# One output projection pass for two mixers, and x added in the attention instead of before it

## The chip, the cores and the metric

The kernel runs on one core of one Trainium2 chip. The metric is the device time of one execution in microseconds (us), less is better. The core's engines are PE (TensorE, matmuls), DVE (VectorE), ACT (ScalarE), POOL (GpSimd) and SP (SyncE, which issues most DMA transfers). Each engine runs its own list of instructions in order and waits on semaphores for the others.

## What is computed

One layer of a hybrid backbone: a modulated norm, one input projection into three mixers (A, differential attention; B, gated linear attention; C, neighbourhood attention), one output projection with a gated residual, a second norm, a mixture of experts and a final norm. What matters here is the residual around the mixers:

```
ya, _ = diff_attention(...)            # 512 columns
yb, _ = gla_mixer(...)                 # 256 columns
yn, _ = neighborhood_attention(...)    # 256 columns
x = x + mod[:, 2] * (jnp.concatenate([ya, yb, yn], axis=-1) @ w_out)
h2 = rms_norm(x, g2) * (1 + mod[:, 4]) + mod[:, 3]
f = hier_moe(h2.reshape(-1, D), w_rg, b_rg, w_re, b_re, w_up, w_down)
x = x + mod[:, 5] * f.reshape(B_, S, D)
return rms_norm(x, final_g)
```

There are 1024 tokens of 1024 numbers, so 8 token tiles of 128 rows. `w_out` is 1024x1024: rows 0 to 511 belong to A, 512 to 767 to B, 768 to 1023 to C.

## The kernel before

**Stages.** Modulation and input projection, mixer B, mixer C, the output projection of B and C (`gen_o`), the attention A with its own part of the output projection, norm, router and token ranking per tile, then the experts, then the final norm. Up to the attention a scheduler sets the order on every engine by what is ready. In the attention and the experts the order on PE, DVE and ACT is written out by hand; SP and POOL stay scheduled there.

**float32 on PE.** Each operand is split into a high and a low part (names in h and l: `mh`, `ml`, `whh`, `whl`), and each product takes three matmuls: high times high, low weight times high, high weight times low.

**The projection before.** `gen_o` (L1066) runs twice. The first run takes mixer B's rows (`mixB`, in the trace `rbm`) with the weights `wB` (`wh`, `wl`, prepared early), the second mixer C's (`mixC`) with `wC` (`whh`, `whl`). In each, per token tile: ACT casts `mh` (L1073), DVE makes `ml` (L1074), and for each of two column halves n PE runs 2 x 3 matmuls of 128x512 (L1079 to L1081) into one of three PSUM buffers `pj`, which DVE adds into `x1` (L1082). `x1` is one SBUF tile of 32 KB per partition that holds x for all 8 tiles, loaded by eight DMAs (L1120) near the end of mixer C. In the second run ACT issues the write of each finished tile to `X1` in device memory (L1084).

**wC.** `wout(768)` (L1053) loads two raw tiles of 512 KB into memory that mixer C has to leave first; for each DVE multiplies by the gate (L1062), ACT casts the high part (L1037), DVE subtracts for the low part (L1034).

**Mixer C's end.** L994 (`cpo`) are its value matmuls, L981 its transposes, L997 the copies into `mixC`.

**The attention.** Units of (tile t, head h), 32 in all. One unit: scores S on PE (L1271, L1272), the row maximum `nm` on DVE (L1273), the exponentials on ACT (L1278), the update of p on DVE (L1284), transposes on PE, values on PE. Work of earlier tiles is woven in with fixed lags: `mixt` loads that tile's X1 rows into `x1t` and forms `mh` and `ml` of A; `proj` (tiles 0 to 6) or `proj_heads` (tile 7) multiplies by A's part of `w_out` and adds into `x1t` (L1368 for tile 7); then the norm, written to `H2` (L1407, POOL), the router, `choose` (small DVE steps up to the one-hot `oh`, L1476), and `rank` (PE, L1488, which reads `oh`). The 30 first steps are a loop; the end is a list written by hand. Buffers named `h2` (in the trace `h`) hold a tile's norm; there are two.

Of the kernel before, what the change touches and what calls it, by code (L numbers as in the profile page):

```python
# [18 lines left out]
D = 1024  # L19
# [3 lines left out]
NT = 8  # L23
# [44 lines left out]
def body(nc, tc, d, tap=None, upto=None):  # L68
# [997 lines left out]
    def gen_o(rows_of, hi, lo, last=False):  # L1066

        o1, x1 = late["o1"], late["x1"]
        for t in range(NT):
            mix = rows_of(t)  # L1070
            mh = o1.tile([128, 2, 128], F32R, name="mh", bufs=2)
            ml = o1.tile([128, 2, 128], F32R, name="ml", bufs=2)
            nc.scalar.copy(mh, mix)  # L1073
            eng(ENG[15]).tensor_sub(ml, mix, mh.bitcast(F32))  # L1074
            for n in range(2):
                cs = slice(512 * n, 512 * n + 512)
                ps = pj.tile([128, 512], F32, name="pj")
                for k in range(2):
                    nc.tensor.matmul(ps, lhsT=mh[:, k, :], rhs=hi[:, k, cs], start=(k == 0), stop=False)  # L1079
                    nc.tensor.matmul(ps, lhsT=mh[:, k, :], rhs=lo[:, k, cs], start=False, stop=False)  # L1080
                    nc.tensor.matmul(ps, lhsT=ml[:, k, :], rhs=hi[:, k, cs], start=False, stop=(k == 1))  # L1081
                nc.vector.tensor_add(x1[:, t, cs], ps, x1[:, t, cs])  # L1082
                if last and n:
                    nc.scalar.dma_start(X1[t * 128:(t + 1) * 128, :], x1[:, t, :])  # L1084
                yield 1.3
# [16 lines left out]
    def last_steps():  # L1102
# [15 lines left out]
        late["x1"] = x1 = O1.enter_context(tc.tile_pool(name="x1", bufs=1)).tile([128, NT, D], F32, name="x1")  # L1118
        for t in range(NT):
            dmab(x1[:, t, :], d["x"][t * 128:(t + 1) * 128, :])  # L1120
# [34 lines left out]
    run(gen_o(lambda t: mixB[:, t], *late["wB"]))  # L1155
    run(gen_o(lambda t: mixC[:, :, t * 128:(t + 1) * 128], *wC, True))
# [6 lines left out]
    if upto == "o1":  # L1163
        nc.sync.dma_start(d["out"], X1)
        A.__exit__(None, None, None)
        Xp.__exit__(None, None, None)
        ctx.close()
        return
# [140 lines left out]
    class Til:  # L1309
# [25 lines left out]
        def mixt(self, a=0, b=4):  # L1335
            if a == 0:
                self.x1 = w2.tile([128, D], F32, name="x1t", bufs=BX1)
                dmab(self.x1, X1[self.t * 128:(self.t + 1) * 128, :])
            pt = apt()
# [14 lines left out]
        def proj_heads(self, ps, n, k0, k1):  # L1354
            cs = slice(512 * n, 512 * n + 512)
            for k in range(k0, k1):
# [14 lines left out]
        def proj(self, n, ps=None):  # L1371
            ps = apt()[:, :256] if ps is None else ps
            cs = slice(256 * n, 256 * n + 256)
# [793 lines left out]
```

## Time and profile before

| what | us |
|---|---|
| median of three runs | 1674.91 (1671.81 to 1677.38) |
| the profiled execution | 1675.7 |
| its span, first to last instruction | 1673.9 |
| mean granted PE clock, as a share of 2.4 GHz | 0.944 |
| PE busy | 1462.1 (87%) |
| DVE busy | 1233.5 (74%) |
| ACT busy | 999.1 (60%) |
| POOL busy | 546.2 (33%) |

The busy shares are means over stages. The projection lies at about 563 to 634 us, the attention at 634 to 930, the experts from about 948 on. The rows that follow further down are from these stretches.

### The profile page before, as it was taken

The numbers are of one execution on the slowest core, as the hardware profiler recorded it, in microseconds if no ns is written. First come the engines' busy times: TensorE is split into PE (matmuls) and PEld (weight loads), VectorE is DVE, ScalarE is ACT, GpSimd is POOL, SyncE is SP. The second block draws the span as 40 slices with busy tenths as digits, with TensorE's granted clock in tenths as the row PEclk, the third lists the DMA queues.
The fourth block names the chain that finished last, engine by engine and source line by source line (L and its number), as shares of the span: only waits on it lengthen the run. The fifth ranks groups of instructions, "written<-read, shape, count | busy, mean of one in ns | idle before, by whom it ended". The sixth has DMA issues, their size and how long they took to land. (4 is left out here: it accounts for less than half of the span.)

```text
span 1673.9 us, 24624 instructions
## 1 busy us (share of the span) xinstructions
PE 1462.1 (87%) x8611; PEld 1193.7 (71%) x8611; DVE 1233.5 (74%) x1936; ACT 999.1 (60%) x1602; POOL 546.2 (33%) x608
## 2 busy tenths in 40 slices
PE   6899799899989897999998689988999999999840
PEld 2698677777777776899998567666777777777730
DVE  5713657965544365867787689998999999999957
ACT  4624546754434523767664377766777777777742
POOL 0201423222322203377885413322222223233224
PEclk9999899999988897999999799999999999999975
DMA  9324572106543686222227789887999999999344
GB/s 325 102 58 137 163 227 67 49 27 186 128 109 96 200 268 244 77 65 89 64 89 273 274 302 337 317 306 261 335 349 344 342 343 344 339 347 340 144 179 192
DMA packets 163502, 353.18 MB, mean 211 GB/s; under 512 B 28247, under 2 KB 83735, under 8 KB 163376
## 3 DMA queue, kind: packets, MB, share of 16 engines
q1 hardware_dynamic: 139552, 307.87, 53.4%
q0 software_dynamic: 22096, 37.94, 7.4%
q10 hardware_dynamic: 1728, 5.78, 0.9%
q8 instruction: 69, 1.13, 0.3%
q14 instruction: 57, 0.47, 0.1%
HBM read 318.30 MB, written 49.30 MB: 220 GB/s over the span
## 5 line engine op out<-in xcount | busy, mean ns | idle before, releaser
L1832 DVE TENSOR_TENSOR wlo<-wraw,whi 128x1024 fp32r<-128x1024 f32 x384 | 505.8, 1338 | 42.8 <-ACT whi L1831 37.7
L1831 ACT CAST whi<-wraw 128x1024 fp32r<-128x1024 f32 x384 | 399.5, 1049 | 160.7 <-PE epu L1859 110.3
L1858 PE MATMUL epu<-wlo,xh 128*128 128x512 f32 x512 | 210.4, 411 | 44.0 <-DVE wlo L1832 42.7
L1857 PE MATMUL epu<-whi,xh 128*128 128x512 f32 x512 | 208.4, 407 | 2.2 <-ACT xh L1849 2.2
L1859 PE MATMUL epu<-whi,xl 128*128 128x512 f32 x512 | 203.9, 398 | 1.0 <-DVE xl L1850 1.0
L1858 PEld LDWEIGHTS epu<-wlo,xh 128*128 128x128 f32 x512 | 97.1, 190 | 89.5 <-DVE wlo L1832 69.3
L1836 POOL DMA_INDIRECT xg<-H,gidx x30 | 42.2, 1407 | 332.2 <-PE ept L1847 320.6
L1877 POOL TENSOR_TENSOR y<-y,m 128x1024 f32<-128x1024 f32 x31 | 88.8, 2865 | 136.2 <-ACT y L1876 136.2
L1273 DVE TENSOR_REDUCE nm<-S 128x1 f32<-128x1280 f32 x64 | 94.9, 1489 | 51.0 <-PE S L1272 42.4
L385 PE MATMUL pj<-wh,hh 128*128 128x256 f32 (+1 forms) x384 | 114.8, 299 | 1.3 <-ACT kbT L342 1.3
L1857 PEld LDWEIGHTS epu<-whi,xh 128*128 128x128 f32 x512 | 97.4, 190 | 24.0 <-ACT xh L1849 2.8
L387 PE MATMUL pj<-wh,hl 128*128 128x256 f32 (+1 forms) x384 | 113.3, 295 | 0.0
L386 PE MATMUL pj<-wl,hh 128*128 128x256 f32 (+1 forms) x384 | 113.3, 295 | 0.0
L1859 PEld LDWEIGHTS epu<-whi,xl 128*128 128x128 f32 x512 | 97.3, 190 | 22.3 <-DVE xl L1850 1.7
L1857 PE MATMUL epy<-whi,ah 128*128 128x512 f32 x256 | 109.0, 426 | 2.3 <-ACT y L1876 2.3
L1858 PE MATMUL epy<-wlo,ah 128*128 128x512 f32 x256 | 102.9, 402 | 0.7 <-DVE wlo L1832 0.7
L1859 PE MATMUL epy<-whi,al 128*128 128x512 f32 x256 | 102.3, 400 | 0.0
L374 PE MATMUL pj<-hh,wh 128*128 128x512 f32 (+1 forms) x240 | 99.9, 416 | 0.0
L1278 ACT ACTIVATE p<-S,nm 128x1280 f32<-128x1280 f32 x64 | 84.6, 1331 | 21.2 <-DMA x1t<-w_out 15.4
L375 PE MATMUL pj<-hl,wh 128*128 128x512 f32 (+1 forms) x240 | 92.1, 384 | 0.0
L376 PE MATMUL pj<-hh,wl 128*128 128x512 f32 (+1 forms) x240 | 91.9, 383 | 0.0
L1271 PE MATMUL S<-ak,aq 128*128 128x512 f32 (+1 forms) x192 | 76.1, 397 | 10.8 <-ACT p L1278 10.0
(447 smaller groups left out, 3513.6 us busy)
## 6 DMA issues: line engine op xcount, KB each, us to landing
wraw<-w_up SPq DMA_DIRECT2D x254, 512.0 KB
wraw<-w_down SPq DMA_DIRECT2D x127, 512.0 KB
wm<-w_mod SPq DMA_DIRECT2D x32, 512.0 KB
raw<-w_in SPq DMA_DIRECT2D x22, 512.0 KB
wm<-w_mod SPq DMA_DIRECT2D x32, 256.0 KB
aq<-QS SPq DMA_DIRECT2D x64, 128.0 KB
wraw<-YS SPq DMA_DIRECT2D x16, 512.0 KB
ak<-KS SPq DMA_DIRECT2D x8, 640.0 KB
```

The lines of the kernel that those rows point to most:

```text
L374: nc.tensor.matmul(ps[:, :n], lhsT=a, rhs=x, start=(k == 0), stop=False)
L375: nc.tensor.matmul(ps[:, :n], lhsT=a, rhs=y, start=False, stop=False)
L376: nc.tensor.matmul(ps[:, :n], lhsT=b, rhs=x, start=False, stop=(k == 7))
L385: nc.tensor.matmul(ps[:, :n], lhsT=a, rhs=wh[:, k, :], start=(k == 0), stop=False)
L386: nc.tensor.matmul(ps[:, :n], lhsT=a, rhs=wl[:, k, :], start=False, stop=False)
L387: nc.tensor.matmul(ps[:, :n], lhsT=b, rhs=wh[:, k, :], start=False, stop=(k == 7))
L1273: V.tensor_reduce(u.nm[:, m:m + 1], sv, axis=AX.X, op=OP.max, negate=True)
L1831: nc.scalar.copy(hi, raw)
L1832: nc.vector.tensor_sub(lo, raw, hi.bitcast(F32))
L1857: nc.tensor.matmul(ps[:, cs], lhsT=ah[:, k, :], rhs=hi[:, cs], start=(k == 0), stop=False)
L1858: nc.tensor.matmul(ps[:, cs], lhsT=ah[:, k, :], rhs=lo[:, cs], start=False, stop=False)
L1859: nc.tensor.matmul(ps[:, cs], lhsT=al[:, k, :], rhs=hi[:, cs], start=False, stop=(k == nk - 1))
```

## The change

The two runs of `gen_o` become one. Per token tile it casts both mixers' rows (`mh` and `ml` are now 128x4x128), and per column half PE runs four steps of three matmuls into one PSUM buffer: two steps with wB, two with wC. The result is copied to a new tile `ev` (two buffers), by ACT for n = 0 and by DVE for n = 1, and ACT writes `ev` to X1. The `x1` tile and its eight loads are gone, so X1 holds the projection without x. In the attention `mixt` loads x of the tile into a buffer of the name `h2` (`xx`), and DVE adds it to `x1t` ahead of the first projection column block: in `proj` for tiles 0 to 6, in `proj_heads` for tile 7. An early exit for tests (`upto == "o1"`) is dropped. In the changed kernel the three matmul lines of `gen_o` are L1083 to L1085, the copies L1086, the write L1087, the adds L1371 (`proj`) and L1351 (`proj_heads`); lines of the attention above them move by a few numbers (L1273 to L1265, L1284 to L1276, L1476 to L1474).

```
-    def gen_o(rows_of, hi, lo, last=False):
-
-        o1, x1 = late["o1"], late["x1"]
+    def gen_o(wB, wC):
+
+        o1 = late["o1"]
         for t in range(NT):
-            mix = rows_of(t)
-            mh = o1.tile([128, 2, 128], F32R, name="mh", bufs=2)
-            ml = o1.tile([128, 2, 128], F32R, name="ml", bufs=2)
-            nc.scalar.copy(mh, mix)
-            eng(ENG[15]).tensor_sub(ml, mix, mh.bitcast(F32))
+            mh = o1.tile([128, 4, 128], F32R, name="mh", bufs=2)
+            ml = o1.tile([128, 4, 128], F32R, name="ml", bufs=2)
+            for z, mix in enumerate((mixB[:, t], mixC[:, :, t * 128:(t + 1) * 128])):
+                zs = slice(2 * z, 2 * z + 2)
+                nc.scalar.copy(mh[:, zs], mix)
+                eng(ENG[15]).tensor_sub(ml[:, zs], mix, mh[:, zs].bitcast(F32))
+            ev = o1.tile([128, D], F32, name="ev", bufs=2)
             for n in range(2):
                 cs = slice(512 * n, 512 * n + 512)
                 ps = pj.tile([128, 512], F32, name="pj")
-                for k in range(2):
-                    nc.tensor.matmul(ps, lhsT=mh[:, k, :], rhs=hi[:, k, cs], start=(k == 0), stop=False)
-                    nc.tensor.matmul(ps, lhsT=mh[:, k, :], rhs=lo[:, k, cs], start=False, stop=False)
-                    nc.tensor.matmul(ps, lhsT=ml[:, k, :], rhs=hi[:, k, cs], start=False, stop=(k == 1))
-                nc.vector.tensor_add(x1[:, t, cs], ps, x1[:, t, cs])
-                if last and n:
-                    nc.scalar.dma_start(X1[t * 128:(t + 1) * 128, :], x1[:, t, :])
-                yield 1.3
+                for k in range(4):
+                    hi, lo = (wB, wC)[k // 2]
+                    h, l = hi[:, k % 2, cs], lo[:, k % 2, cs]
+                    nc.tensor.matmul(ps, lhsT=mh[:, k, :], rhs=h, start=(k == 0), stop=False)
+                    nc.tensor.matmul(ps, lhsT=mh[:, k, :], rhs=l, start=False, stop=False)
+                    nc.tensor.matmul(ps, lhsT=ml[:, k, :], rhs=h, start=False, stop=(k == 3))
+                (nc.vector.tensor_copy if n else nc.scalar.copy)(ev[:, cs], ps)
+            nc.scalar.dma_start(X1[t * 128:(t + 1) * 128, :], ev)
...
-        late["x1"] = x1 = O1.enter_context(tc.tile_pool(name="x1", bufs=1)).tile([128, NT, D], F32, name="x1")
-        for t in range(NT):
-            dmab(x1[:, t, :], d["x"][t * 128:(t + 1) * 128, :])
...
-    run(gen_o(lambda t: mixB[:, t], *late["wB"]))
-    run(gen_o(lambda t: mixC[:, :, t * 128:(t + 1) * 128], *wC, True))
+    gen_o(late["wB"], wC)
...
                 self.x1 = w2.tile([128, D], F32, name="x1t", bufs=BX1)
                 dmab(self.x1, X1[self.t * 128:(self.t + 1) * 128, :])
+                self.xx = w2.tile([128, D], F32, name="h2", bufs=BH2)
+                dmab(self.xx, d["x"][self.t * 128:(self.t + 1) * 128, :])
...
         def proj_heads(self, ps, n, k0, k1):
             cs = slice(512 * n, 512 * n + 512)
+            if k0 == n == 0:
+                V.tensor_add(self.x1, self.x1, self.xx)
...
         def proj(self, n, ps=None):
             ps = apt()[:, :256] if ps is None else ps
             cs = slice(256 * n, 256 * n + 256)
+            if n == 0:
+                V.tensor_add(self.x1, self.x1, self.xx)
```

**PE at the end of mixer C.** The names: `cpo` is mixer C's output, `wh` and `wl` are wB, `whh` and `whl` are wC, `mh` and `ml` the mixers' rows, `pj` the PSUM buffers. The kernel before:

```order
L1079 MATMUL pj_5813<-wh_5063,mh_5801 128x512
L1080 MATMUL pj_5813<-wl_5064,mh_5801 128x512
L994 MATMUL cpo_5718<-cpT_5708,vw_5582 64x128
L994 MATMUL cpo_5718<-cpT_5716,vw_5582 64x128
L1081 MATMUL pj_5813<-wh_5063,ml_5802 128x512
L994 MATMUL cpo_5718<-cpT_5708,vw_5582 64x128
L994 MATMUL cpo_5718<-cpT_5716,vw_5582 64x128
L1079 MATMUL pj_5825<-wh_5063,mh_5821 128x512
L994 MATMUL cpo_5718<-cpT_5708,vw_5582 64x128
L994 MATMUL cpo_5718<-cpT_5716,vw_5582 64x128
L1080 MATMUL pj_5825<-wl_5064,mh_5821 128x512
L1081 MATMUL pj_5825<-wh_5063,ml_5822 128x512
```

The same place in the changed kernel:

```order
L994 MATMUL cpo_5706<-cpT_5696,vw_5570 64x128
L994 MATMUL cpo_5706<-cpT_5704,vw_5570 64x128
L1083 MATMUL pj_5776<-whh_5723,mh_5769 128x512
L1083 MATMUL pj_5790<-whh_5723,mh_5769 128x512
L1083 MATMUL pj_5812<-whh_5723,mh_5805 128x512
L1084 MATMUL pj_5776<-whl_5724,mh_5769 128x512
L1085 MATMUL pj_5776<-whh_5723,ml_5770 128x512
L1083 MATMUL pj_5776<-whh_5723,mh_5769 128x512
```

Before, B matmuls of one PSUM buffer after another stand between and behind mixer C's last matmuls; now the first projection matmuls behind them read wC, and 18 B matmuls stand further ahead, in both programs.

**DVE in a unit of the attention.** `nm` is the row maximum and factor, `p0` the probabilities, `fm`, `eid`, `oh`, `tB` belong to `choose` of an earlier tile. The kernel before:

```order
L1284 SCALAR_TENSOR_TENSOR p0_7715<-p1_7717,nm_7680,p0_7715 128x1280
L1469 TENSOR_TENSOR fm_7747<-fm_7747,iot_5519 128x32
L1472 TENSOR_SCALAR fm_7747<-fm_7747,eid_5522 128x32
L1473 TENSOR_SCALAR oh0_7870<-iot_5519,eid_5522 128x32
L1449 ISA fm_7747,eid_5522<-fm_7747 128x32
L1449 ISA eid_5522 128x1
L1475 TENSOR_SCALAR tB0_7872<-iot_5519,eid_5522,cid_6178 128x32
L1476 TENSOR_SCALAR oh1_7871<-iot_5519,eid_5522 128x32
L1273 TENSOR_REDUCE nm_7894<-S0_6195 128x1
```

The same place in the changed kernel, where the tile's x lies in `h2_7719`:

```order
L1276 SCALAR_TENSOR_TENSOR p0_7671<-p1_7673,nm_7636,p0_7671 128x1280
L1371 TENSOR_TENSOR x1t_7717<-x1t_7717,h2_7719 128x1024
L1467 TENSOR_TENSOR fm_7703<-fm_7703,iot_5519 128x32
L1470 TENSOR_SCALAR fm_7703<-fm_7703,eid_5522 128x32
L1471 TENSOR_SCALAR oh0_7829<-iot_5519,eid_5522 128x32
L1447 ISA fm_7703,eid_5522<-fm_7703 128x32
L1447 ISA eid_5522 128x1
L1473 TENSOR_SCALAR tB0_7831<-iot_5519,eid_5522,cid_6125 128x32
L1474 TENSOR_SCALAR oh1_7830<-iot_5519,eid_5522 128x32
```

The add stands between the update of p and the steps that end with `oh`. It stands so for tiles 2 to 5; for tiles 0 and 1 no `choose` step follows it, and for tile 6 it stands between the maxima and the update of p.

**SP at the attention's end.** `x1t` is tile 7's load of X1, `wraw` are raw weights of the experts, `h2` in the changed kernel tile 7's x. The kernel before:

```order
L77 DMA x1t_9248<-X1_68 128x1024
L1894 DMA wraw_9629<-w_down 128x1024
L1894 DMA wraw_9631<-w_down 128x1024
L1894 DMA wraw_9633<-w_down 128x1024
L1894 DMA wraw_9635<-w_down 128x1024
L1894 DMA wraw_9637<-w_up 128x1024
```

The changed kernel:

```order
L77 DMA x1t_9216<-X1_68 128x1024
L1892 DMA wraw_9600<-w_down 128x1024
L1892 DMA wraw_9602<-w_down 128x1024
L1892 DMA wraw_9604<-w_down 128x1024
L1892 DMA wraw_9606<-w_down 128x1024
L77 DMA h2_9218<-x 128x1024
L1892 DMA wraw_9608<-w_up 128x1024
```

The load of tile 7's x stands behind four loads of `w_down` and ahead of the next of `w_up`.

## Rows read from the trace of the kernel before

**Rows 1.** Timeline of PE at the end of mixer C and in the projection: start in us, busy us, engine, line, operation, output<-inputs, tile and shape, count, and in brackets the idle time before and what ended it. Between the rows of 591.83 and 600.03 stand 34 more matmuls of this kind.

```profile
557.52 0.77 PE L981 MATMUL cps<-ident,cs 128*128 128x128 f32 x5
563.46 0.79 PE L1079 MATMUL pj<-wh,mh 128*128 128x512 f32 x1 [5.17 <-ACT mh L1073]
...
588.16 0.50 PE L1079 MATMUL pj<-wh,mh 128*128 128x512 f32 x1
...
591.12 0.44 PE L994 MATMUL cpo<-cpT,vw 128*64 128x128 f32 x4
...
591.83 0.40 PE L1081 MATMUL pj<-wh,ml 128*128 128x512 f32 x1
...
600.03 0.40 PE L1080 MATMUL pj<-wl,mh 128*128 128x512 f32 x1
...
603.18 0.47 PE L1079 MATMUL pj<-wh,mh 128*128 128x512 f32 x1 [1.31 <-DVE x L1082]
...
633.00 0.40 PE L1081 MATMUL pj<-whh,ml 128*128 128x512 f32 x1
```

**Rows 2.** Waits of SP's queue from 585 to 606 us (line, what it waited for: us in total, times, longest) and, from the timeline of SP, the issue that ended the wait.

```profile
SPq L77 <- PE cpo L994: 7.9, 1, 7.9
...
591.72 0.81 SPq L77 DMA_DIRECT2D raw<-w_out  x2
```

**Rows 3.** Timeline of DVE from mixer C's last copy to the attention's first maxima, columns as in rows 1.

```profile
591.61 0.29 DVE L997 COPY mixC<-cpo 128x128 f32<-128x128 f32 x1 [0.16 <-PE cpo L994]
...
595.78 0.69 DVE L1082 TENSOR_TENSOR x<-pj,x 128x512 f32<-128x512 f32 x1 [0.39 <-PE pj L1081]
596.39 1.22 DVE L1062 TENSOR_TENSOR raw<-raw 128x1024 f32<-128x1024 f32 x1
...
598.12 1.22 DVE L1062 TENSOR_TENSOR raw<-raw 128x1024 f32<-128x1024 f32 x1
...
601.20 1.23 DVE L1034 TENSOR_TENSOR whl<-raw,whh 128x1024 fp32r<-128x1024 f32 x1
...
633.44 0.69 DVE L1082 TENSOR_TENSOR x<-pj,x 128x512 f32<-128x512 f32 x1 [0.71 <-PE pj L1081]
641.83 2.89 DVE L1273 TENSOR_REDUCE nm<-S 128x1 f32<-128x1280 f32 x2 [7.70 <-DMA X<-x]
```

**Rows 4.** Timeline of ACT: the first cast of wC, and the last three issues of X1 writes (one row, its time is that of all three with the waits between them).

```profile
597.68 1.06 ACT L1037 CAST whh<-raw 128x1024 fp32r<-128x1024 f32 x1 [0.33 <-DVE raw L1062]
...
628.54 5.97 ACTq L1084 DMA_DIRECT2D X<-x  x3
```

**Rows 5.** Windows of the projection and of the attention's start: from:to and length in us, then busy us and instruction count of PE, PE's weight loads, DVE, ACT and POOL, the granted PE clock as a share of 2.4 GHz, the share of DMA busy, and GB/s.

```profile
560.00:564.00 4.00, 0.55 (x1) 0.50 (x2) 1.08 (x4) 2.91 (x8) 1.75 (x4) 0.70 0.57 132
592.00:596.00 4.00, 4.00 (x18) 3.22 (x18) 1.93 (x4) 0.41 (x1) 0.00 (x0) 1.00 0.69 254
600.00:604.00 4.00, 1.99 (x8) 1.02 (x7) 3.57 (x6) 1.17 (x2) 0.00 (x0) 1.00 1.10 347
636.00:640.00 4.00, 0.78 (x5) 0.48 (x3) 0.00 (x0) 0.00 (x0) 1.08 (x1) 1.00 1.02 420
640.00:644.00 4.00, 0.00 (x0) 0.00 (x0) 2.17 (x2) 0.60 (x1) 0.00 (x0) 0.51 1.03 418
644.00:660.00 16.00, 11.94 (x37) 9.83 (x38) 9.58 (x8) 6.41 (x11) 9.34 (x4) 0.50 0.67 244
...
656.00:660.00 4.00, 4.00 (x17) 3.62 (x16) 1.13 (x2) 1.41 (x3) 0.00 (x0) 0.50 0.42 172
660.00:664.00 4.00, 4.00 (x30) 3.70 (x30) 3.04 (x5) 3.97 (x8) 0.00 (x0) 0.93 0.00 0
```

**Rows 6.** Window of one unit in the middle of the attention, columns as in rows 5.

```profile
759.90:768.25 8.35, 8.31 (x64) 7.63 (x63) 5.72 (x13) 6.03 (x15) 7.09 (x16) 1.00 0.11 43
```

**Rows 7.** Timeline of DVE in that unit, columns as in rows 1.

```profile
762.76 1.57 DVE L1284 SCALAR_TENSOR_TENSOR p<-p,nm,p 128x1280 f32<-128x1280 f32 x1
...
765.10 0.23 DVE L1476 TENSOR_SCALAR oh<-iot,eid 128x32 f32<-128x32 f32 x1
767.50 1.49 DVE L1273 TENSOR_REDUCE nm<-S 128x1 f32<-128x1280 f32 x1 [2.17 <-PE S L1272]
```

**Rows 8.** Timeline of PE in that unit: the rank matmuls and the scores behind them.

```profile
765.54 0.61 PE L1488 MATMUL S<-oh,tri 128*128 128x32 f32 x4
765.99 0.48 PE L1271 MATMUL S<-ak,aq 128*128 128x512 f32 x1
```

**Rows 9.** Windows at the attention's end, columns as in rows 5: the first lies in one of the last units, the second in tile 7's projection.

```profile
892.00:896.00 4.00, 4.00 (x36) 3.79 (x34) 3.96 (x16) 3.70 (x9) 2.79 (x4) 1.00 0.91 362
...
920.00:924.00 4.00, 4.00 (x25) 3.48 (x24) 0.68 (x2) 0.00 (x0) 3.92 (x2) 1.00 1.03 420
```

**Rows 10.** Timeline of DVE ahead of tile 7's first add (L1368), columns as in rows 1.

```profile
919.17 0.16 DVE L104 SCALAR_TENSOR_TENSOR r<-r 128x1 f32<-128x1 f32 x1
922.74 0.19 DVE L1505 TENSOR_TENSOR acc<-apt,acc 128x32 f32<-128x32 f32 x1 [3.41 <-PE apt L1504]
923.52 0.69 DVE L1368 TENSOR_TENSOR x1t<-S,x1t 128x512 f32<-128x512 f32 x1 [0.58 <-DMA wraw<-w_up]
```

**Rows 11.** Timeline of POOL: the issue of tile 5's H2 write.

```profile
908.42 0.62 POOL L1407 DMA_DIRECT2D H<-h  x1 [0.30 <-POOL h L1406]
```

**Rows 12.** Timeline of SP: the four loads of `w_down` behind tile 7's X1 load.

```profile
905.79 5.15 SPq L1894 DMA_DIRECT2D wraw<-w_down  x4
```

More of the change, by code (lines that the diff above doesn't have):

```diff
@@ L1162, in body @@
     PJ.__exit__(None, None, None)
[L1163 to L1168, printed above, removed]
     xp, kk, va = late["xp"], late["kk"], late["va"]
```

## The prediction, on record before the changed kernel ran

> **What bounds the kernel now.** I read the windows around the output projection first, then the lists of single instructions there, then one unit of the attention, then the attention's end. Three things are to be seen.
>
> First, the place of the projection. The last mixer-C matmuls stand between 588.16 and 591.3 with five B matmuls of the projection among them [rows 1]. They free mixer C's memory, and SP issues the two loads of wC at 591.72, having waited for just that [rows 2]. From there wC takes DVE and ACT until 602.4: multiply at 596.39 and 598.12, ACT cast at 597.68, the low parts up to 601.20 + 1.23 [rows 3, 4]. PE does not wait for it: it runs B matmuls from 591.83 to 600.03 without a gap, 35 pitches in 8.20 us, so 0.2343 us each, and only 2 us of gap follow before 603.18 [rows 1, 5]. B's matmuls are the cover for wC. The last projection matmul starts at 633.00 [rows 1], the last add at 633.44 [rows 3].
>
> Second, what follows. The attention's first max at 641.83 has waited 7.70 us for the last X1 write [rows 3], which ACT issued as the third of three at about 634.1 [rows 4]. PE stands idle meanwhile.
>
> Third, the attention. PE is busy 8.31 of 8.35 us in a unit, DVE 5.72, ACT 6.03, POOL 7.09 [rows 6]: PE is the bound, and DVE waits for scores once per unit, 2.17 us [rows 7]. Behind it the MoE starts from the routed tokens and repeats the same order, so I let a shift at the attention's end stand to the kernel's end.
>
> **The projection.** It has 192 matmuls before and after, so the work is the same and only the order counts. Three PSUM buffers hold three groups; in the new program a group is finished only with wC. So 18 B matmuls can run before wC, and PE's order shows exactly 18 of them. Of the old program the same 18 stood ahead of 588.16, so in both 174 matmuls remain from there. The old ones fill the wait for wC; the new ones stand behind it.
>
> When is wC ready in the new order? Without the five B matmuls the last mixer-C matmuls follow at once: three groups of four, 0.44 us each with pipelining [rows 1], end near 589.1 in place of 591.5. The raw loads then go at 589.2, 2.5 us sooner. How long they take is only bounded: the window 592 to 596 moved 4 us x 254 GB/s = 1.0 MB, both raws, so the first lands at earliest some 3.0 us after its issue; the multiply at 596.39 gives at most 4.7 [rows 3, 5]. I take 3.2, since DVE was held by an L1082 add right up to that multiply [rows 3]: 592.4. Multiplies of 1.22 end at 593.6 and 594.8, the first cast of 1.06 [rows 4] at 594.7, the second low part at 597.3. PE starts on wC at about 594.7, has six of the 174 matmuls done at 597.3, and the other 168 x 0.2343 = 39.4 us end at 636.7, against 633.00 + 0.23 = 633.2 now: **+3.4** before the clock.
>
> The clock. PE would stand idle from 589.1 to 594.7, 5.6 us. The trace has that twice: idle from the start of the last row at 557.52 plus its 0.77 to 563.46, after which the matmuls take 0.79 in place of 0.40 [rows 1] in a window whose mean is 0.70 [rows 5]; and idle after 636.8, when 636 to 640 is still at 1.00 and 640 to 644 at 0.51 [rows 5]. The level is 1.2 GHz then, half of 2.4. It comes back late: PE is busy 4.00 us in 656 to 660 at 0.50 and only 660 to 664 has 0.93 [rows 5], so at least 4 us of full work pass at half pace. I take 4 us, 2.0 lost: **+2.0**, projection **+5.4** in all. Bounds: +3.4 if the clock holds, +8 if the raws take 4.7 (+1.5) and mixer C's end gains 1 us less.
>
> The rule that speaks against this change is the Trainium skill's, page "TensorE: Matmul & The Clock Gate", section "Loop structure matters more than you think": a DMA wait inside a matmul loop lets the array go cold, so work should be ordered to have none. By that rule the term is +5.4, without it +3.4; the two stretches just read agree with it.
>
> The copies to ev (ACT for n = 0, DVE for n = 1) cost no path: one per 12 x 0.2343 = 2.8 us group, and the nearest rows are 0.69 us [rows 3]. The dropped adds were as long. An ev buffer comes free when its X1 write has landed: the longest seen is 7.7 us [rows 3, 4], the distance to the next use three groups, 8.4 us; with that cover gone the three PSUM buffers still give some 5 us, so nothing.
>
> **The last X1 write.** Its 7.7 us [rows 3] were shared with loads of w_up and w_out at 420 GB/s [rows 5]. In the new order SP has three w_up loads there, not four, and 512 KB at 420 GB/s is 1.25 us. **-1.0**, between 0 and -3.
>
> **The added adds, tiles 2 to 5.** Each is 128x1024 from two SBUF tiles: 1.22 us by L1062, the same form [rows 3]. In these four units the order puts it between the p update (L1284) and the choose steps that end with oh (L1476), ahead of seven small steps. Now oh ends at 765.10 + 0.23 and PE's rank matmuls, which need it, start at 765.54 [rows 7, 8], 0.2 us later. With 1.22 in between PE waits 1.0 us, and PE has 0.04 us of slack in a unit [rows 6]; behind the rank matmuls stand the next scores on PE. 4 x 1.0 = **+4.0**. Bounds: 0 if PE comes later than DVE anyway, 4.9 if nothing is hidden. In tiles 0 and 1 no choose step stands there; the add falls into the 2.17 us in which DVE waits for scores [rows 7]: 0, at most 1.
>
> **Tile 6.** The add stands between the maxima and the p update of a unit where DVE is busy 3.96 of 4.00 us and PE 4.00 [rows 9]. **+1.0**, 0 to 1.3.
>
> **Tile 7.** DVE is idle from 919.33 to 922.74 ahead of L1368 at 923.52 [rows 10], so 1.22 us fit if x has landed by about 922. Its load now shares a buffer with the norm of tile 5, so it waits for the H2 write issued at 908.42 [rows 11] and stands on SP behind four w_down loads, the block that took from 905.79 to 910.94 [rows 12]. With DMA 0.9 to 1.0 busy around here [rows 9] I estimate 918 to 926. **+1.0**, 0 to 6. SP's w_up loads behind it start some 2 us later, and the MoE needs them 25 us later. The other x loads and all x1t loads are tiles ahead of use; the 4 MB of x no longer loaded at the end of mixer C cost nothing there, since neither PE nor DVE waited for them [rows 1, 3].
>
> **Sum.** 5.4 - 1.0 + 4.0 + 1.0 + 1.0 = +10.4. The profiled execution took 1675.7 us (span 1673.9), 0.8 above the median of 1674.91: 1675.7 + 10.4 = **1686.1**. About 0.3%, 5 us, is what a measurement of this kernel can tell from no change.
>
> **Rivals.** *The write lands in time* (not slower). If SP's loads don't stand in front of the last X1 write, the first max comes some 3 us after it, not 7.7, and PE starts again in the stretch that still had 1.00 after the scores, up to 640 [rows 5]. That gives 4.7 us less the 1.0 already taken, and the 16 us from 644 to 660, now at 0.50 with 11.94 busy, would run at 2.4 GHz: up to 6 us. 1686.1 - 3.7 - 6 = 1676. What decides is whether the write lands within some 3 us of its issue. Against it: w_out's loads wait for the same end of the projection as the write, and 636 to 644 moved 420 GB/s [rows 5]. Chance 0.1.
>
> *The clock holds and the adds are covered.* PE's wait for wC is cut by sooner raws and PE reaches the rank matmuls late: 1675.7 + 3.4 - 1 = 1678. For it: 0.2 us decide the four units. Against it: two idles of this length that did lower the clock. Chance 0.14.
>
> *Tile 7's x comes late and nothing is hidden.* 1675.7 + 5.4 - 1 + 4.9 + 1.3 + 6 = 1692, or 1695 with the projection at +8. Chance 0.14.
>
> *It does not do what it says.* The new order still has to wait for wC, but if mixer C, freed of x's loads and of its four L1082 adds (4 x 0.69 = 2.8 us) [rows 3], ended sooner by all of these, wC would come 2.8 us sooner, the idle before it would stay the same length, and the projection's term would fall to +2.6: 1683, within the forecast. To end faster than before it takes this together with the first two rivals: 1676 - 2.8 - 4 = 1669. Chance 0.04.
>
> **How the numbers follow.** The forecast (1680 to 1691) has 0.58. Slower by over 0.3% are the forecast, the late x (0.14) and 0.04 of the two rivals that end near no change: 0.76. Within 0.3% is the rest of these two: 0.20. Faster is the last: 0.04. All low ends together give 1676, all high ones 1696; 8 in 10 is 1677 to 1695.
>
> **What would show it.** The last projection matmul starts at 637 to 641; PE is idle 5 to 6 us ahead of the first whh matmul and the window after it shows a clock under 1.00; the raw loads go 2 to 3 us sooner; rank matmuls wait 1 us for DVE in four units and L1371 has 7 rows of about 1.22 us; L1351 starts by 922 plus the shift. Wrong would be a gap ahead of whh under 3 us, an ev copy that waits for DMA, or a first max within 4 us of the last X1 write.

## The result, and the profile of the changed kernel

The changed kernel takes 1687.08 us (median of five runs, 1683.75 to 1688.55), the kernel before 1674.91 (five runs, 1671.81 to 1677.38). The ratio is 1.0078 with a 95% interval of 1.0063 to 1.0092: slower by 12.2 us, 10.5 to 15.4 by the interval. The forecast was 1686.1, slower.

The profiled execution of the changed kernel took 1688.55 us, span 1686.5, clock 0.944. It already stands 4.45 us behind at the first `mh` cast of the projection (567.45 against 563.00), in a part of the program whose code the change does not touch. The same cast stood at 563.0 to 568.5 us in the other profiles of this study, and at 566.8 us in a second profile of the kernel before, so I measure each step from a mark inside it.

PE's timeline of the changed kernel, columns as in [rows 1]: the end of mixer C, the first matmul on wC, the last of the projection, and the rank matmuls of one unit.

```profile
593.67 0.92 PE L994 MATMUL cpo<-cpT,vw 128*64 128x128 f32 x11
...
601.02 1.65 PE L1083 MATMUL pj<-whh,mh 128*128 128x512 f32 x3 [6.43 <-ACT whh L1037]
...
643.37 0.39 PE L1085 MATMUL pj<-whh,ml 128*128 128x512 f32 x1
...
773.85 0.87 PE L1486 MATMUL S<-oh,tri 128*128 128x32 f32 x4 [0.34 <-DVE oh L1471]
```

Where [rows 1] show PE at work on B matmuls while wC is made, PE now stands idle for 6.43 us, and the three matmuls behind that take 1.65 us together; where the clock holds (e10_raw_early below) the same three take 0.96. The rank matmuls, which came 0.2 us behind `oh` without a wait [rows 7, 8], wait for it. DVE's timeline of the same kernel:

```profile
598.54 2.36 DVE L1062 TENSOR_TENSOR raw<-raw 128x1024 f32<-128x1024 f32 x2 [3.62 <-DMA raw<-w_out]
...
652.71 2.89 DVE L1265 TENSOR_REDUCE nm<-S 128x1 f32<-128x1280 f32 x2 [8.22 <-DMA X<-ev]
...
662.58 1.55 DVE L1276 SCALAR_TENSOR_TENSOR p<-p,nm,p 128x1280 f32<-128x1280 f32 x1
...
772.05 1.21 DVE L1371 TENSOR_TENSOR x1t<-x1t,h 128x1024 f32<-128x1024 f32 x1
...
774.02 0.23 DVE L1474 TENSOR_SCALAR oh<-iot,eid 128x32 f32<-128x32 f32 x1
...
930.20 1.23 DVE L1351 TENSOR_TENSOR x1t<-x1t,h 128x1024 f32<-128x1024 f32 x1
933.65 0.19 DVE L1503 TENSOR_TENSOR acc<-apt,acc 128x32 f32<-128x32 f32 x1 [2.23 <-PE apt L1502]
```

The raw loads were issued at 594.73 and the first multiply came 3.8 us later (I had taken 3.2, between 3.0 and 4.7). The first max still waits for the last X1 write. Tile 7's add lies in idle time of DVE, as does the wait behind it. The windows, columns as in [rows 5], show the clock:

```profile
592.00:596.00 4.00, 2.59 (x24) 1.74 (x23) 0.29 (x1) 0.69 (x1) 0.20 (x1) 1.00 0.31 96
596.00:600.00 4.00, 0.00 (x0) 0.00 (x0) 1.46 (x2) 0.08 (x1) 0.00 (x0) 0.75 0.93 351
600.00:604.00 4.00, 2.98 (x7) 2.22 (x8) 3.26 (x3) 1.98 (x2) 0.00 (x0) 0.50 1.06 346
604.00:608.00 4.00, 4.00 (x17) 3.16 (x17) 1.36 (x3) 1.89 (x4) 0.00 (x0) 0.90 1.07 355
...
656.00:660.00 4.00, 3.99 (x12) 3.06 (x11) 1.49 (x1) 1.21 (x3) 4.00 (x2) 0.57 0.46 181
660.00:664.00 4.00, 1.43 (x6) 1.05 (x6) 3.76 (x4) 2.67 (x4) 2.52 (x2) 1.00 0.48 135
```

The clock falls in the idle time (0.75 in 596 to 600, 0.50 in 600 to 604) and is back within 604 to 608 (0.90). The last two lines hold something that the prediction had not: at the attention's start the clock is back 8 us after the first max, where the kernel before waited about 18 [rows 5].

### The profile page after: what moved, and what is told of

Same layout as the page of the kernel before. It is cut to its first block, busy times and chain, and to the rows that moved or that the text cites. A ratio compares the mean times of both kernels' runs of the same rounds, so it can differ in the third digit from the quotient of the medians.

```text
span 1686.5 us, 24612 instructions
## 1 busy us (share of the span) xinstructions
PE 1461.7 (87%) x8611; PEld 1193.4 (71%) x8611; DVE 1228.0 (73%) x1920; ACT 1003.4 (59%) x1610; POOL 554.4 (33%) x608
## 5 line engine op out<-in xcount | busy, mean ns | idle before, releaser
L1265 DVE TENSOR_REDUCE nm<-S 128x1 f32<-128x1280 f32 x64 | 94.8, 1488 | 45.6 <-PE S L1264 37.4
```

What stands on the lines that cost most here:

```text
L1265: V.tensor_reduce(u.nm[:, m:m + 1], sv, axis=AX.X, op=OP.max, negate=True)
```

## The experiments

"First cast" is the first `mh` cast of the projection, "mixer C's end" the end of its last value matmul (`cpo`), "xl" the first expert step. A unit has two row maxima, so the seventh reduction opens the last of units 0 to 3, and unit 4 begins with the ninth. Ratios are to the kernel before, run in turn with each. Of each edit the main lines are shown.

| kernel | median us (runs) | ratio, 95% interval |
|---|---|---|
| changed kernel | 1687.08 (5) | 1.0078, 1.0063 to 1.0092 |
| e1_merge_only | 1678.62 (12) | 1.0019, 1.0002 to 1.0037 |
| e2_adds_only | 1677.74 (12) | 1.0011, 0.9993 to 1.0028 |
| e3_add_moved | 1685.62 (6) | 1.0062, 1.0042 to 1.0082 |
| e4_wc_early | 1674.66 (12) | 0.9994, 0.9979 to 1.001 |
| e5_early_add_behind | 1675.28 (12) | 1.0003, 0.9986 to 1.002 |
| e6_early_ev_aside | 1675.15 (12) | 1.0005, 0.9987 to 1.0023 |
| e7_early_x_at_evict | 1686.44 (6) | 1.0067, 1.0042 to 1.0092 |
| e8_early_both | 1685.2 (9) | 1.005, 1.0027 to 1.0073 |
| e9_x_ahead | 1670.36 (12) | 0.9974, 0.9955 to 0.9993 |
| e10_raw_early | 1680.08 (12) | 1.0021, 1.0003 to 1.0038 |
| e12_pool_longer | 1687.37 (6) | 1.0073, 1.0051 to 1.0095 |

**The two halves of the change.** e1_merge_only keeps `x1` and its early loads and only merges the passes:

```
-                (nc.vector.tensor_copy if n else nc.scalar.copy)(ev[:, cs], ps)
-            nc.scalar.dma_start(X1[t * 128:(t + 1) * 128, :], ev)
+                nc.vector.tensor_add(x1[:, t, cs], ps, x1[:, t, cs])
+            nc.scalar.dma_start(X1[t * 128:(t + 1) * 128, :], x1[:, t, :])
```

> Merged pass of four steps, but x stays preloaded in the 32 KB tile and is added there; nothing is added in the attention. If the wait of PE for wC behind the merged order is the larger part of the loss, PE is idle about 6 us ahead of the first whh matmul, the projection ends 5 to 8 us later than in the kernel before, no rank matmul waits for DVE, and the total is 1678 to 1683 us. If the added adds in the attention are the larger part, the total is within 2 us of the kernel before (1673 to 1677).

e2_adds_only keeps the two passes, without x, and adds x in the attention:

```
-                nc.vector.tensor_add(x1[:, t, cs], ps, x1[:, t, cs])
+                if last:
+                    nc.vector.tensor_add(x1[:, t, cs], ps, x1[:, t, cs])
+                else:
+                    nc.vector.tensor_copy(x1[:, t, cs], ps)
```

> The two passes of the kernel before, but without x (the first pass copies out of PSUM, the second adds), and x loaded and added per tile in the attention. If the adds cost what the trace of the changed kernel shows (0.8 us at each of five tiles), the projection ends as before, four rank matmuls wait some 0.3 us for oh and start 0.8 us later each, and the total is 1677 to 1680 us. If the wait for wC is all of the loss, the total is 1673 to 1676.

Measured +3.3 and +2.4 us (the intervals reach from 0.3 to 6.2 and from -1.2 to 4.7), each in the first of its two expected ranges, and together 5.7, against 12.2 for both. The traces show each term larger: from mixer C's end to the last projection matmul e1 takes 49.0 us (before 41.4), and from unit 4 to xl e2 takes 284.0 us (before 279.0). Taken away from the changed kernel, the halves are worth more as well: 8.5 us the adds (1687.08 less e1), 9.3 us the order (1687.08 less e2). In their profiles both e1 and e2 gained some 3 us in units 0 to 3, which the sum counts twice; e11 and e12 below are about that. The other half of the missing 6.5 us stays open.

**The add moved in its unit.** e3_add_moved puts the add behind the first half of `choose`, so that it is not between the p update and `oh`:

```
-            if n == 0:
-                V.tensor_add(self.x1, self.x1, self.xx)
...
             todo["mixt"].mixt()
             todo["mixt"].low()
+            V.tensor_add(todo["mixt"].x1, todo["mixt"].x1, todo["mixt"].xx)
```

> The changed kernel with the add of x moved behind the choose steps, at the end of the iteration ahead. If the add's place on DVE ahead of oh is what holds PE, the rank matmuls start as in the kernel before and the total falls by 3 to 4 us against the changed kernel (1683 to 1684). If PE is late for another reason, such as more DVE work in all, the total stays within 1 us of the changed kernel.

1685.62, between the two expected ranges and not distinguishable from the changed kernel. DVE's timeline shows why:

```profile
762.65 1.23 DVE L1584 TENSOR_TENSOR x1t<-x1t,h 128x1024 f32<-128x1024 f32 x1
763.79 2.88 DVE L1265 TENSOR_REDUCE nm<-S 128x1 f32<-128x1280 f32 x2
...
769.36 0.23 DVE L1472 TENSOR_SCALAR oh<-iot,eid 128x32 f32<-128x32 f32 x1
```

The maxima now follow the add without a gap and are late themselves, and `oh` with them. From the first half of `choose` to `oh` DVE has no slack; its idle time lies behind `oh`. The three units around such an add (15 to 17) still take 0.8 us more than in the kernel before (25.4 us, 24.6), nearly as much as in the changed kernel (0.9).

**wC made earlier.** e4_wc_early is the changed kernel with wC loaded and split during mixer C, in memory that `x1` held before:

```
+        late["o3"] = O1.enter_context(tc.tile_pool(name="o3", bufs=1))
+        late["wC"] = wout(768)
...
-    wC = wout(768)
```

> The changed kernel with wC loaded and split during mixer C, into the memory that the x tile leaves free, so that the merged pass waits for nothing of mixer C's memory. If the wait for wC and the slow clock behind it are the loss in the projection, PE is not idle at mixer C's end, the projection ends 8 to 12 us sooner than in the changed kernel, and the total is 1675 to 1680 us. If the split of wC on DVE and ACT now delays mixer C as much, or the loss lies in the wait for the last X1 write, the total is within 3 us of the changed kernel.

1674.66: 12.4 us below the changed kernel, the time of the kernel before. No idle time stands before wC, and from the first cast to the last projection matmul it takes 67.2 us, where the changed kernel takes 75.9. So 8.8 of the 12.4 us are seen in this stretch. It scatters by several us between profiles of one form (63.2 to 68.9 in e4 to e6, 72.9 to 77.4 in the four that wait for wC), and the rest lies within what the two intervals leave open.

e10_raw_early moves only the two raw loads:

```
+        late["raw"] = [o1.tile([128, D], F32, name="raw", bufs=2) for k in range(2)]
+        for k in range(2):
+            dmab(late["raw"][k], d["w_out"][768 + 128 * k:768 + 128 * k + 128, :])
...
-            raw = o3.tile([128, D], F32, name="raw", bufs=2)
-            dmab(raw, d["w_out"][row + 128 * k:row + 128 * k + 128, :])
+            raw = late["raw"][k]
```

> The changed kernel with one thing moved: the two loads of wC's rows are issued during mixer C, into memory that x held before; the multiplication by the mask, the split and everything behind them stay where they are. This parts the wait for wC into the transfer (3.8 us from issue to the first multiplication) and the split behind it. Theory: the wait is the sum of both, so the first matmul with whh starts 2.5 to 4 us after the end of mixer C and not 6.4, the idle time is too short to lose the clock for as long, and the time is 3 to 7 us below that of the changed kernel (1680 to 1684 us). Rival one: the casts of the split on ScalarE are late by themselves, behind mixer C's last copies, and the transfer was hidden behind them; then less than 1 us is gained. Rival two: the slow clock in 596 to 604 us costs more than the wait and goes whole with the shorter wait; then nearly all of the 12 us come back (1674 to 1677 us).

1680.08, 7.0 us below the changed kernel. PE's timeline and two windows:

```profile
587.82 0.92 PE L994 MATMUL cpo<-cpT,vw 128*64 128x128 f32 x11
589.99 0.96 PE L1082 MATMUL pj<-whh,mh 128*128 128x512 f32 x3 [1.26 <-ACT whh L1037]
591.25 0.50 PE L1083 MATMUL pj<-whl,mh 128*128 128x512 f32 x1 [0.30 <-DVE whl L1034]
```

```profile
588.00:592.00 4.00, 2.45 (x18) 1.64 (x15) 2.32 (x3) 2.00 (x2) 0.20 (x1) 1.00 1.10 357
592.00:596.00 4.00, 4.00 (x18) 3.22 (x18) 1.69 (x4) 1.78 (x4) 0.00 (x0) 1.00 1.07 348
```

With transfer and multiply out of the way 1.26 us of wait are left, the clock stays at 1.00, and from the end of mixer C to the last projection matmul it takes 42.5 us, not 48.8. The idle time fell by 5.2 us and the stretch by 6.3: 1.2 us of it is the clock. Against the other profiles of the changed order (e1, e3, e12: idle 6.37 to 6.81 us, 49.0 to 50.2 us in all) it is 1.5 to 2.2 us.

**The add behind oh.** e5_early_add_behind is e4 with the add behind `oh`, where DVE is idle; the first piece of A's projection is added after it:

```
+        if "p0" in todo:
+            todo["p0"].plus_x()
```

> wC early, as in the run before it (1674.7 us), and for tiles 0 to 5 the add of x stands behind the choose steps that end with oh, in the same iteration, where DVE next waits 1.8 us for scores; POOL's first add of the tile comes behind it. If only DVE's stretch up to oh has no slack, the rank matmuls start as in the kernel before and the total falls by 3 to 4 us, to 1671 to 1672. If DVE has no slack anywhere in the unit, the total stays at 1674 to 1676.

1675.28, no gain, as in the second of the two expectations. In the units of tiles 2 to 4 (16, 20 and 24) the wait for `oh` is gone: they take 8.42 to 8.44 us as in the kernel before (8.43, 8.44), where the changed kernel takes 9.19 to 9.22. But the next unit takes 10.1 us and not 8.6. One such place, from the timelines of DVE, POOL and PE:

```profile
796.44 0.85 DVE L1273 SCALAR_TENSOR_TENSOR nm<-nm,ls,ss 128x1 f32<-128x1 f32 x1
797.32 3.76 DVE L1274 SCALAR_TENSOR_TENSOR p<-p,nm,p 128x1280 f32<-128x1280 f32 x1
```

```profile
797.35 2.38 POOL L1409 TENSOR_TENSOR h<-h,m3r 128x1024 f32<-128x1024 f32 x1
```

```profile
801.23 1.06 PE L1282 MATMUL apt<-ident,p 128*128 128x128 f32 x8 [1.02 <-DVE rk L1452]
```

The same place in e4:

```profile
804.96 2.36 DVE L1273 SCALAR_TENSOR_TENSOR nm<-nm,ls,ss 128x1 f32<-128x1 f32 x1
807.36 1.55 DVE L1274 SCALAR_TENSOR_TENSOR p<-p,nm,p 128x1280 f32<-128x1280 f32 x1
```

```profile
804.95 2.37 POOL L1402 TENSOR_TENSOR h<-h,m3r 128x1024 f32<-128x1024 f32 x1
```

In both, DVE meets POOL's second norm multiply. In e4 the small step ahead of the p update pays for it (2.36 us; 0.22 us a unit earlier), in e5, in the sooner phase, the p update itself (3.76 us), and the two steps together take 4.64 us from start to end in place of 3.95. Behind them the two steps `tA` take 1.46 us, beside POOL's adds into `x1t`, and 0.55 us in e4. That is about the 1.5 us of this unit, and PE waits for DVE.

**The X1 write out of the way.** e6_early_ev_aside is e4 with `ev` in memory that the attention's first unit does not take:

```
-            ev = o1.tile([128, D], F32, name="ev", bufs=2)
+            ev = late["ov"].tile([128, D], F32, name="ev", bufs=2)
```

> wC early, and ev in other memory, so that the attention's first tiles don't reuse it and the first max doesn't wait for the last X1 write. If that wait holds the attention's start, the first max comes within 3 us of the last projection matmul instead of 9, PE's clock stays at 2.4 GHz there, and the total falls by 6 to 11 us, to 1664 to 1669. If the attention waits next for something as late (the loads of w_out, the first exponentials' memory), the total stays within 2 us of 1674.7.

1675.15, no gain, as in the second of the two expectations, though the start went as meant: the first max stood 2.7 us after the last projection matmul (9.0 in e4), and PE's clock stayed at 1.00 until the wait in the second row of DVE's timeline:

```profile
638.44 2.89 DVE L1266 TENSOR_REDUCE nm<-S 128x1 f32<-128x1280 f32 x2 [1.59 <-PE S L1265]
...
660.77 1.49 DVE L1266 TENSOR_REDUCE nm<-S 128x1 f32<-128x1280 f32 x1 [5.02 <-PE S L1265]
```

The memory wait moved: now the gate for w_out (`hT`) and w_out's rows need the memory of `ev`. The waits of SP's queue from 630 to 656 us have it (columns as in [rows 2]):

```profile
SPq L77 <- DMA X<-ev: 8.1, 1, 8.1
```

SP issued w_out's rows at 646.06, 14 us later than in e4 (632.20), POOL got them at 652.96, ACT's cast of `wah` waited 2.5 us for POOL, and the fourth unit lost 3.9 us (11.9 against 8.0 in e4). This was the prediction's first rival (a write that lands in time): the wait can be removed, but the loads behind it then become the wait. That is not all of it: in the profiles the stretch from the last projection matmul to unit 4 is still 5.9 us shorter than in e4 (30.4 and 36.3 us). The medians show nothing of this, and why stays open.

**x at the eviction.** e7_early_x_at_evict is e4 with x loaded per tile in `gen_o` and added there by DVE, without the adds in the attention; e8_early_both has e6's `ev` as well.

```
+            xin = o1.tile([128, D], F32, name="xin", bufs=2)
+            dmab(xin, d["x"][t * 128:(t + 1) * 128, :])
...
-                (nc.vector.tensor_copy if n else nc.scalar.copy)(ev[:, cs], ps)
+                nc.vector.tensor_add(ev[:, cs], ps, xin[:, cs])
```

> wC early, and x loaded per tile into two small buffers and added by DVE when the PSUM result is taken out, in place of the copies; no add in the attention. If the adds in the attention cost 5 us in all, as the distances from the first max to the first expert step show, the total is 1669 to 1671. If SP, which now waits for these buffers, or DVE delays the projection as much, the total stays at 1674 to 1677.

> The last two together: x added at the eviction and ev in other memory. If the two terms are independent, the total is their sum below 1674.7: 1659 to 1665 us. If both work through PE's idle time at the attention's start, it is no lower than the better of the two by more than 2 us.

1686.44 and 1685.2, some 11 us lost, so neither expectation held (at most 1677 for e7, 1665 for e8's sum). SP's and PE's timelines of e7:

```profile
592.91 7.22 SPq L77 DMA_DIRECT2D aq<-QS  x4
600.18 1.22 SPq L77 DMA_DIRECT2D xin<-x  x2
```

```profile
608.77 0.80 PE L1085 MATMUL pj<-wh,mh 128*128 128x512 f32 x1 [15.11 <-DVE ev L1088]
```

The first x loads stand on SP behind the loads for the attention, and PE waits 15.11 us for the first evictions. In e8 it waits 15.21 us at the same place.

e9_x_ahead mends that: four `ev` buffers hold x, loaded ahead in mixer C for the first four tiles.

```
+        late["ev"] = [x_of(t) for t in range(4)]
...
-            ev = o1.tile([128, D], F32, name="ev", bufs=2)
+            ev = late["ev"][t] if t < 4 else x_of(t)
...
-                (nc.vector.tensor_copy if n else nc.scalar.copy)(ev[:, cs], ps)
+                nc.vector.tensor_add(ev[:, cs], ps, ev[:, cs])
```

> The merged pass with wC split during mixer C (as in e4_wc_early), but with x added at the eviction again and no add in the attention: four eviction buffers hold x before the add, the first four tiles of x loaded during mixer C, where the kernel before loads all of x. My theory is that e7_early_x_at_evict lost its 15 us because the first x loads stood on SP behind the loads of ak, av and aq, so that TensorE waited 15.1 us for the first evictions. Then here the last projection matmul starts within 1 us of where it does in e4_wc_early (67.2 us after the first cast of mh), the attention is 4 to 5 us shorter than in e4_wc_early, and the time is 1669 to 1672 us, faster than both kernels. Rival: the loads of tiles 4 to 7 wait for the X1 write of tiles 0 to 3 on a busy DMA and stall TensorE again, or they hold SP and so the loads that the attention's start needs; then the last projection matmul starts more than 3 us later, or the attention's first units are later, and the time is 1675 or more.

1670.36, by the ratio 4.4 us below the kernel before (1.2 to 7.5) and 16.7 below the changed one. PE runs the projection without a wait; first cast to last matmul takes 68.8 us (1.6 more than in e4, where 1 was allowed), and unit 4 to xl takes 278.7. Against e4, which differs in where x is loaded and added, the median is 4.3 us lower (each has some 3 us of uncertainty) and this last stretch 5.3 us shorter: the price of the adds, a second time.

**Units 0 to 3.** e11_before_again is the kernel before, unedited, for a second profile (one run, 1681.48 us).

> The kernel before without a change, for a second profile. The first profile of it had 21.9 us from the first to the seventh reduction of the attention (units 0 to 3), and every other kernel of this series 15.8 to 19.3 us, because TensorE's clock came back later. If that is chance of one execution, this profile shows 16 to 20 us there and up to 4 us less in the span; if it belongs to the kernel before, it shows 21 to 22 us again. It also shows how far the same instructions ahead of the projection scatter: the first cast of mh stood at 563.0 us, and at 563.5 to 568.5 us in the other kernels.

The seventh reduction stood 22.3 us after the first again (21.9 in the first profile), so it is no chance of one execution. DVE and POOL there:

```profile
658.84 3.60 DVE L1284 SCALAR_TENSOR_TENSOR p<-p,nm,p 128x1280 f32<-128x1280 f32 x1
```

```profile
656.43 4.67 POOL L1027 TENSOR_TENSOR h<-h,hT 128x1024 f32<-128x1024 f32 x2
```

Beside POOL's multiplies of w_out's rows the first p update takes 3.60 us. In every edited kernel so far no such multiply was under way then, and it took 1.55. The range of 15.8 to 19.3 us leaves out e8: there the second p update met one and took 3.62 us, and the seventh reduction stood 20.8 us after the first. e12_pool_longer forces the meeting in the changed kernel by a second, unused product per row block:

```
-            wout_load(128 * i, raws[i], m2b)
+            dmab(raws[i], d["w_out"][128 * i:128 * i + 128, :])
+            nc.gpsimd.tensor_mul(wal[:, i, :], raws[i], m2b)
+            nc.gpsimd.tensor_mul(raws[i], raws[i], m2b)
```

> The changed kernel with GpSimd's four multiplications of w_out's rows at the attention's start done twice (the extra product goes to wal, which is overwritten later), so that GpSimd is busy there some 18.7 us instead of 9.3. The results are those of the changed kernel. In both profiles of the kernel before, the first p update (from S, nm and p, 128x1280 on VectorE) took 3.60 us and lay beside such a multiplication; in all ten profiles of other kernels so far it took 1.55 us and GpSimd had ended before it. Theory: this overlap, which the change removes by chance of timing, is what gave 4 us back at the attention's start. Then here the first p update takes about 3.6 us again, the second perhaps too, TensorE's clock comes back later, the seventh reduction stands 20 to 23 us after the first (17.45 in the changed kernel), and the time is 2 to 6 us above the changed kernel's, 1689 to 1693. Rival: the late clock alone made the difference and the long p update was its companion; then the p update takes 1.55 us beside GpSimd, the seventh reduction stands 17 to 19 us after the first, and the time is 1685 to 1688.

```profile
659.35 3.60 DVE L1276 SCALAR_TENSOR_TENSOR p<-p,nm,p 128x1280 f32<-128x1280 f32 x1
```

```profile
659.26 2.34 POOL L1560 TENSOR_TENSOR wal<-h,hT 128x1024 fp32r<-128x1024 f32 x1
661.68 3.48 POOL L1561 TENSOR_TENSOR h<-h,hT 128x1024 f32<-128x1024 f32 x1
```

In the profile the theory holds: 3.60 us again, the clock back late, the seventh reduction 22.6 us after the first (17.5 in the changed kernel). In the medians it does not show: 1687.37 against 1687.08, where the two intervals together leave some 4 us open either way. Half of the expectation fell. In the changed kernel's profile POOL's last multiply ends at 662.52 (657.83 + 4.69) and the p update starts at 662.58; with so little between them other executions may well have met. That is argued, not shown: only one execution was profiled.

## Why the prediction was right

The sign and the two causes were right, and the sum came near: 10.4 us forecast, 12.2 measured. That it came so near is in part luck: the X1 write gave nothing, tile 1's add cost 0.9 us where nothing was forecast, tile 6's cost nothing where 1.0 was, and units 0 to 3, for which the prediction had no term, became shorter in the profile. By terms, with profiles of the same form taken together:

| term | forecast us | measured us |
|---|---|---|
| projection: first cast to last matmul | +5.4 | +4.3 |
| last X1 write: to the first max | -1.0 | +0.2 |
| adds, unit 4 to xl | +6.0 | +5.2 |
| units 0 to 3 | none | -4.0 in the profile, open in the median |
| sum | +10.4 | +9.7 without units 0 to 3 |

The two profiled executions differ by 12.6 us in span (1673.9 and 1686.5): 4.45 stand ahead of the first cast, 5.9 in the projection, 0.5 up to the first max, -4.0 in units 0 to 3, 5.3 from there to xl and 0.3 behind it. So 8.1 us lie in parts that the change reaches, and the first 4.45 are scatter as far as the profiles show.

**The projection.** From the first cast: 70.0 and 73.1 us (e11) in the kernel before; with the changed order 75.9, 77.4 (e1), 72.9 (e3) and 77.3 (e12). The means differ by 4.3. e2, with the old order but without the loads of x, takes 65.4, so a single pair proves little. The scatter lies ahead of mixer C's end, which stands 22.0 to 30.1 us behind the first cast in these seven. Behind it the rows are firm: 41.4, 43.0 and 43.5 us (e2) in the old order, 48.8 to 50.2 in the new one, so 6.8 us more, where the prediction's numbers give 7.9 (49.4 against 41.5). The chain is the predicted one: mixer C's end frees the memory, the raws take 3.8 us, the split the rest, PE idles 6.43 us (6.37 to 6.81 in e1, e3 and e12; 5.6 was forecast), and the clock goes. The clock cost about what was taken for it, 2.0: from the first matmul on wC to the last it takes 42.4 to 43.4 us, in e10 at a clock of 1.00 41.2, so 1.2 to 2.2 us. The loop-structure rule of the Trainium skill ("TensorE: Matmul & The Clock Gate", "Loop structure matters more than you think") agrees: 0.50 after the wait here, 1.00 throughout in e10 where the wait was 1.26 us.

Two readings were off. Not five but seven B matmuls stand among mixer C's last ones, and three groups of 0.44 us from 588.16 end at 589.5, not 589.1. The 2.5 us by which mixer C was to end sooner can't be read from these: it ended 26.5 us after the first cast in the mean of the new order and 29.3 in the two profiles of the kernel before, but 22.0 in e2, which keeps the old order. That the loads of x cost nothing there is not shown either: with all eight of them the stretch is 28.4 to 30.1 us (before, e11, e1), without them 22.0 to 27.1 (changed, e2, e3, e12). By medians e4 puts the price of the wait at 12.4 us and e10 that of transfer and multiply at 7.0, more than the profiles show; each has an uncertainty of 3 to 4 us.

**The X1 write.** This step failed, by 1 us. From the last matmul to the first max: 8.8 and 8.4 us before, 9.3, 8.4, 9.2 and 8.3 after (changed, e1, e3, e12). The write is still issued among w_out's loads: at 644.57, between loads at 644.17 and 645.11, and DMA moved 380 GB/s from 648 to 652.

**The adds.** From unit 4 to xl the profiles without adds (before, e1, e7, e8, e9, e11) take 278.6 to 279.0 us, those with them in the predicted place or e3's (changed, e2, e3, e4, e10, e12) 283.2 to 284.5: +5.2. Unit by unit the kernel before and the changed one differ only at the adds, in us:

| units | add of tile | before | changed |
|---|---|---|---|
| 8 and 9 | 0 | 14.69 | 14.69 |
| 12 and 13 | 1 | 15.74 | 16.62 |
| 16 and 17 | 2 | 16.91 | 17.82 |
| 20 and 21 | 3 | 16.92 | 17.80 |
| 24 and 25 | 4 | 16.92 | 17.83 |
| 28 and 29 | 5 | 19.06 | 19.93 |
| 30 | 6 | 9.08 | 9.08 |

Tiles 2 to 5 cost 0.9 us each, where 1.0 was forecast, and e5 shows that 0.8 of it is the wait for `oh`. Tile 1 cost as much, by a way that the prediction did not have. Its add falls into idle time of DVE as forecast, but POOL's small step beside it takes 1.06 us and not 0.19, POOL's norm multiplies come 0.87 us later in the unit, and DVE's next p update, which meets the second of them in both kernels, comes later by as much (the step ahead of it is held for 1.32 us, 0.46 before). e2, e4, e10 and e12 show the same (unit 13: 8.65 to 8.67 us, before 7.79, changed 8.66); no run moved this add alone. DVE and POOL in the changed kernel:

```profile
738.54 1.21 DVE L1371 TENSOR_TENSOR x1t<-x1t,h 128x1024 f32<-128x1024 f32 x1
744.74 1.32 DVE L1275 SCALAR_TENSOR_TENSOR nm<-nm,ls,ss 128x1 f32<-128x1 f32 x1
746.10 3.75 DVE L1276 SCALAR_TENSOR_TENSOR p<-p,nm,p 128x1280 f32<-128x1280 f32 x1
```

```profile
738.75 1.06 POOL L101 TENSOR_TENSOR r<-r 128x1 f32<-128x1 f32 x1
746.13 2.38 POOL L1404 TENSOR_TENSOR h<-h,m3r 128x1024 f32<-128x1024 f32 x1
```

And in the kernel before:

```profile
737.80 0.46 DVE L1283 SCALAR_TENSOR_TENSOR nm<-nm,ls,ss 128x1 f32<-128x1 f32 x1
738.29 3.74 DVE L1284 SCALAR_TENSOR_TENSOR p<-p,nm,p 128x1280 f32<-128x1280 f32 x1
```

```profile
731.81 0.19 POOL L101 TENSOR_TENSOR r<-r 128x1 f32<-128x1 f32 x1
738.32 2.37 POOL L1406 TENSOR_TENSOR h<-h,m3r 128x1024 f32<-128x1024 f32 x1
```

Tile 6's add, put at 1.0, cost nothing. Tile 7's x came in time, so the late-x rival did not occur, and its add, put at 1.0 too, did not delay the first projection add behind it (35.7 us after the first max of unit 31, 36.2 before). Up to xl 0.9 us are lost all the same; where behind that add, and why, stays open.

**Units 0 to 3.** The prediction had no term for them, and the traces show one. In the profiles it also hid some 3 us of the cost in each of e1 and e2. What it is worth in the changed kernel's median stays open: the three terms sum to 9.7, the measurement says 12.2 (10.5 to 15.4), which leaves no room for a gain, and e12's median shows none.

## What to carry to other kernels

When two passes are merged into one accumulation, look at what the first pass was covering: its matmuls may be the only work while the second pass's weights are made, and the memory that the merge frees can hold those weights sooner. Work added to an engine that is idle on average is paid almost in full if it stands ahead of the instruction that the bound engine waits for; moved elsewhere, or even in idle time of its own engine, it can still hold up another engine and be paid for a unit later. Before taking away a wait on a reused buffer, look at what will take that memory instead.

## What was not expected of the hardware

In these traces a VectorE instruction that reads SBUF twice and a GpSimd one that does too did not run beside each other: 128x1280 takes 1.55 us alone, and 3.60 (before, e11, e12), 3.62 (e8) or 3.74 to 3.76 (e5 and the place of tile 1 above) where it meets a GpSimd multiply of 2.34 to 2.38; in e12 the next GpSimd multiply took 3.48 us in turn, not 2.34 to 2.37. A small one is held as well: 128x1 took 2.36 us in e4 and not 0.22. The Trainium skill, page "SBUF — State Buffer", section "Who interferes with whom", says that a VectorE instruction with two SBUF inputs contends with a GpSimd one that reads SBUF, and that contention on the port pair they share is an exclusive lock. The rows agree: 1.55 + 2.34 = 3.89 would be the full wait.

The clock's return shifted with it: in the three profiles where the first p update took 3.60 us the seventh reduction stood 21.9, 22.3 and 22.6 us after the first, in e8, where the second one was held, 20.8, in the others 15.8 to 19.3. Which of the two brings the other is not shown.
